# Gate projections of a hybrid diffusion layer moved in between the convolution tiles, and kept in DRAM until their merges

## The chip, the cores and the metric

The kernel is one program on one core of a Trainium2 chip. The metric is the device time of one execution in microseconds (us). Every time of an instruction below is from one profiled execution.

## The reference

Two token streams, 128 context tokens and 512 latent tokens, pass two layers with shared weights (D = 1024). Here both are one array of T = 640 columns. A layer is

```
h  = rmsnorm(x) * (1 + sc1) + sh1
proj = h @ w_in                       # q, k, v, z, b, a, the convolution's 3 x 512, Fourier's 512, 3 gates x 1024
y_a = delta_mixer(proj[q,k,v], z, b, a)         # gated DeltaNet, forward and backward, chunks of 64
y_b = hyena_mixer(proj[3 x 512])                # two long convolutions in the spectrum, gated
y_c = fourier_mixer(proj[512])                  # real part of a 2-D Fourier transform per group
g   = sigmoid(proj[gates])                      # three gates per channel
x  += g1 * ((g[0] * (y_a @ w_pa) + g[1] * (y_b @ w_pb) + g[2] * (y_c @ w_pc)) @ w_o)
x  += g2 * swiglu(rmsnorm(x) * (1 + sc2) + sh2)
```

and one last rmsnorm ends it. The outputs are both streams and the context's DeltaNet states.

## The kernel before

Activations lie transposed, 128 channels on the partitions and 640 tokens in the columns. A projection tile is 128 output channels: `gemm` makes it in two halves of 320 columns, each of 8 k-steps of three matmuls (the fp32 operands are split into a high and a low part, `mm3`), so 48 matmuls, into a PSUM tile named `pg`. Its weights come by one 512 KB load `wr` and are split into `wh` by ACT and `wl` by POOL (`wsplit`). A merge takes weights for two output tiles; a branch has four merges, 192 matmuls.

The source writes the foreground (projections, merges) as a plain sequence and everything else as coroutines (`bg`). After each quarter of a tile `pump` lets those coroutines issue a step whose inputs are ready by a cost model's clock; `finish` runs coroutines until they are done, with nothing of the foreground between. Each engine then executes its own list in that fixed order. SP issues nearly all transfers, in its own fixed order too.

In a layer's mixer (`mixer`) the order before is, after q, k and v: the delta block (`delta`: three batches of a triangular inverse on DVE, then the scan) starts in the background. The foreground is 4 Fourier tiles, stored to `fnS`; 4 z tiles, stored to `zS`; 12 convolution tiles (`proj_conv`: besides the matmuls four ACT copies and two DVE operations of 641 columns, stored to `hyS`); 8 gate tiles of branch a. I call this stretch the mix. Then `delta_out` (norm of the delta block's output, product with z) runs in the background of two gate tiles of branch c. Then the a merges with `fnet` (Fourier) in the background; the c merges with the other 6 c gates between them and `hyena` in the background; the 8 b gates, still with `hyena`; the b merges. I call the stretch from `delta_out` to the first b merge the tail. `hyena` is four passes (two halves of the channels, two orders): transposes, then five spectral stages, each with its own table load from `hT` and filter load from `kSp`, PE forward, DVE products, PE inverse; then two gated products.

The large SBUF tiles `A` come from a pool of 14, `T` (656 columns) from 6, `U` from 8.

Of the kernel before, what the change touches and what calls it, by code (L numbers as in the profile page):

```python
# [18 lines left out]
P = 128  # L19
D = 1024  # L20
# [4 lines left out]
T = TP + TS  # L25
NC = T // 2
# [14 lines left out]
OFF_HY = 2080  # L41
OFF_FN = 3616
OFF_G = 4128
QKV_ORDER = (4, 5, 6, 7, 0, 1, 2, 3, 8, 9, 10, 11)
BR = {"a": 0, "b": 1, "c": 2}
C_BMOD, C_G1, C_G2, C_CQ, C_CH, C_NA, C_FQ, C_B1, C_B2, C_NF = 0, 48, 56, 64, 100, 136, 137, 138, 139, 140
NPAR = 148


def _stream():  # L50
    s = [("ba", 0)] + [("in", m * P) for m in QKV_ORDER]
    s += [("in", OFF_FN + m * P) for m in range(4)]
    s += [("in", 1536 + m * P) for m in range(4)]
    s += [("in", OFF_HY + m * P) for m in range(12)]
    gate = lambda br, m: ("in", OFF_G + BR[br] * D + m * P)
    s += [gate("a", m) for m in range(8)]
    s += [gate("c", 0), gate("c", 1)]
    s += [("pa", m) for m in range(0, 8, 2)]
    s.append(("pc", 0))
    for m in range(2, 8, 2):  # L60
        s += [gate("c", m), gate("c", m + 1), ("pc", m)]
    s += [gate("b", m) for m in range(8)]
    s += [("pb", m) for m in range(0, 8, 2)]
# [235 lines left out]
class _Net:  # L299
# [138 lines left out]
                self.room -= c["pe"] - p  # L438
        self.last_pe = c["pe"]

    def finish(self, *cos):
        while True:
            cos = [co for co in cos if not co.done]
            if not cos:
                return
            self.finish_one(cos)

    def finish_one(self, cos):

# [193 lines left out]
    def setup(self):  # L643
        nc, I = self.nc, self.I
        sm = self.kp.tile([P, 1024], F32, name="small")
        nc.sync.dma_start(sm, I["small"])
        self.ident = sm[:, 0:128]
        self.ones = sm[:, 128:256]
        self.mask = sm[:, 256:384].rearrange("p (s i) -> p s i", s=2)
        self.inc = sm[:, 384:640].rearrange("p (s i) -> p s i", s=2)  # L650
        self.stc = sm[:, 640:896].rearrange("p (s i) -> p s i", s=2)
        self.parity = sm[:, 896:1024].rearrange("p (s i) -> p s i", s=2)
        sr = self.kp.tile([P, 256], F32R, name="stcr")
        nc.vector.tensor_copy(sr, sm[:, 640:896])
# [8 lines left out]
        self.hT = self.dr.tile([5, P, 2048], F32, name="hT")  # L663

    def load_par(self, l):
        nc = self.nc
# [387 lines left out]
    def proj_conv(self, key, wcol, l):  # L1054

        W = self.wget(key)
        cv = self.conv_tile(wcol, l)
        for c in range(2):
            self.proj(W, cv, c)
        return self.conv(cv)  # L1060

    def permute(self, dst, src, fn, goff=1):

# [668 lines left out]
            yield  # L1732


    def gates(self, l, br, dst):

        for m in range(8):
            self.gate(l, br, m, dst[m // 4][:, m % 4])

    def gate(self, l, br, m, dst):  # L1740
        W = self.wget(("in", OFF_G + BR[br] * D + m * P))
        for c in range(2):
            self.evict(dst, self.gemm(W, self.h, c, free=2), c, AF.Tanh, 0.5)
            self.pump()

    def merge(self, br, m, th, first, last):

        nc = self.nc
        W = self.wget(("p" + br, m))
        for i in range(2):  # L1750
            mt = self.mg[(m + i) // 4][:, (m + i) % 4]
# [21 lines left out]
    def mixer(self, l, co):  # L1773
        nc = self.nc
        v4 = lambda a: a.rearrange("p (m t) -> p m t", m=4)
# [11 lines left out]
        W = {}  # L1787
        for c in range(2):
# [3 lines left out]
            ps = self.gemm(W[-1], self.h, c, M=32, free=((1, 0), (0, 1))[c])  # L1792
# [29 lines left out]
        for m in range(4):  # L1822
            W = self.wget(("in", OFF_FN + m * P))
            t = self.Tt()
            for c in range(2):
                self.evict(t, self.gemm(W, self.h, c, free=2), c)
                self.pump()
            nc.sync.dma_start(self.fnS[m], t[:, :T])
        par = self.par[l][0]
        na = self.p2.tile([P, 1], F32, tag="na2", name=self.nm("na2"))  # L1830
        nc.vector.tensor_scalar(out=na, in0=par[:, C_NA:C_NA + 1], scalar1=0.5, scalar2=None, op0=ALU.mult)
        for m in range(4):
            W = self.wget(("in", 1536 + m * P))
            t, zm = self.Tt(), self.Tt()
            for c in range(2):
                ps = self.gemm(W, self.h, c, free=2)
                self.evict(t, ps, c, AF.Tanh, 0.5)
                sl = slice(c * NC, (c + 1) * NC)
                nc.vector.scalar_tensor_tensor(out=zm[:, sl], in0=t[:, sl], scalar=1.0, in1=ps[:, :NC],
                                               op0=ALU.add, op1=ALU.mult)  # L1840
                self.pump()
            nc.gpsimd.tensor_scalar(out=zm[:, :T], in0=zm[:, :T], scalar1=na, scalar2=1.0, op0=ALU.mult, op1=ALU.mult)
            nc.sync.dma_start(self.zS[m], zm[:, :T])
        self.mark(f'hy{l}')
        for m in range(12):
            o = self.proj_conv(("in", OFF_HY + m * P), C_CH + 3 * m, l)
            nc.sync.dma_start(self.hyS[m][:, 0:641], o)
        self.mark(f'ga{l}')
        while self.dst() is None:
            self.finish_one(gd)  # L1850
        self.mg = [v4(self.A()) for _ in range(2)]
# [12 lines left out]
        gh = self.bg(self.after(gf, self.hyena(l)))  # L1864
        mgv = [self.mg[m // 4][:, m % 4] for m in range(8)]
        for m in range(0, 8, 2):
            self.merge("a", m, mgv[m:m + 2], True, False)
        self.y["a"] = None
        self.mark(f'c{l}')
# [12 lines left out]
        self.h = None  # L1882
        self.mark(f'hfin{l}')
        self.finish(gh)
        self.mark(f'pb{l}')
        self.mgs = [[v4(self.A(F32R)) for _ in range(2)] for _ in range(2)]
        self.gm = self.bg(self.mods(l, (38, 40)[l], 48))
        for m in range(0, 8, 2):
            self.merge("b", m, [tb[(m + i) // 4][:, (m + i) % 4] for i in range(2)], False, True)
# [312 lines left out]
```

## Time and profile before

| | |
|---|---|
| median of 3 runs (lowest, highest) | 2847.31 us (2843.88, 2851.53) |
| profiled execution | 2847.94 us, of it 2846.2 us from the first to the last instruction |
| busy share | PE 91%, PEld 86%, DVE 66%, POOL 47%, ACT 36% |
| DMA | 324.24 MB, mean 114 GB/s |
| mean granted TensorE clock | 0.955 |

A line of the page or of an answer names tiles without their numbers: `pg` is a projection's or a merge's sum, `ps` any other PSUM tile, `hT`, `kSp`, `hyS`, `zS`, `fnS` are DRAM tensors. PE is the matmul itself, PEld its weight load. A granted clock of 1.00 is 2.4 GHz, and 0.5 is 1.2 GHz.

### The profile page before, as it was taken

The page shows a single profiled execution, that of the slowest core. Times are in us where ns is not written, and L with a number is a line of the kernel's source. Part 1 is how long each engine was busy: PE and PEld are TensorE (multiplying, and loading weights), DVE is VectorE, ACT ScalarE, POOL GpSimd, SP SyncE. Part 2 cuts the span into 40 slices and gives each one's busy share as a digit, 9 for nine tenths or more (in the row PEclk, how much of TensorE's full clock was granted, in tenths as well). Part 3 has the DMA queues.
Part 4 walks back from the last instruction along what each step waited for, and adds up shares of the span by engine and source line. Part 5 has one row for each costly group of instructions (what it writes and reads, how often), then busy time and mean ns, then how long its engine had stood idle before and what let it go on. Part 6 is the DMA issues. An engine that isn't in the chain of part 4 may idle for free. (4 is left out here: it accounts for less than half of the span.)

```text
span 2846.2 us, 56258 instructions
## 1 busy us (share of the span) xinstructions
PE 2595.5 (91%) x22664; PEld 2455.5 (86%) x22664; DVE 1870.7 (66%) x3504; ACT 1030.8 (36%) x2235; POOL 1331.2 (47%) x1228
## 2 busy tenths in 40 slices
PE   5798879898999999999988988799899999999998
PEld 3677778898999989999987777688889989999997
DVE  4466897844654585667765779876556457877765
ACT  2445223332233243344425542333323323444432
POOL 1242535333334465566633444354423345767662
PEclk9899989999999999999999999899999999999999
DMA  7432122243564336422222322213336442222222
GB/s 277 165 99 93 61 85 66 78 139 120 186 241 135 112 98 202 139 83 82 82 99 80 108 85 72 78 57 97 109 140 232 157 163 62 73 82 82 82 75 82
DMA packets 99957, 324.24 MB, mean 114 GB/s; under 512 B 10842, under 2 KB 25178, under 8 KB 93216
## 3 DMA queue, kind: packets, MB, share of 16 engines
q1 hardware_dynamic: 98256, 312.76, 33.2%
q0 software_dynamic: 1440, 7.87, 0.8%
q8 instruction: 179, 2.93, 0.4%
q14 instruction: 82, 0.67, 0.1%
HBM read 288.60 MB, written 37.24 MB: 114 GB/s over the span
## 5 line engine op out<-in xcount | busy, mean ns | idle before, releaser
L2151 PE MATMUL pg<-A,wh 128*128 128x320 f32 (+1 forms) x6304 | 1477.1, 321 | 53.7 <-DVE T L2151 14.8
L2151 PEld LDWEIGHTS pg<-A,wh 128*128 128x128 f32 (+1 forms) x6304 | 1081.6, 194 | 107.5 <-issue 22.3
L2151 POOL TENSOR_TENSOR wl<-wr,wh 128x512 fp32r<-128x512 f32 (+2 forms) x486 | 677.5, 1407 | 777.5 <-ACT wh L2151 745.4
L2151 PE MATMUL pg<-A,wl 128*128 128x320 f32 (+1 forms) x3152 | 997.9, 317 | 0.5 <-POOL wl L2151 0.4
L2151 PEld LDWEIGHTS pg<-A,wl 128*128 128x128 f32 (+1 forms) x3152 | 610.7, 194 | 3.6 <-POOL wl L2151 2.6
L2151 ACT CAST wh<-wr 128x512 fp32r<-128x512 f32 (+2 forms) x486 | 286.7, 612 | 416.1 <-PE pg L2151 306.7
L2151 PE MATMUL ps<-A,wh 128*128 128x320 f32 x1696 | 379.6, 310 | 0.0
L2151 PEld LDWEIGHTS ps<-A,wh 128*128 128x128 f32 x1696 | 283.4, 188 | 3.4 <-issue 2.4
L2151 PE MATMUL ps<-A,wl 128*128 128x320 f32 x848 | 263.6, 311 | 4.6 <-POOL wl L2151 4.3
L2151 PE MATMUL ps<-A,A 32*32 32x32 f32 (+5 forms) x2984 | 214.0, 249 | 51.7 <-DVE A L2151 50.0
L2151 POOL TENSOR_TENSOR wl<-U,wh 128x512 fp32r<-128x512 f32 x160 | 225.9, 1425 | 52.9 <-ACT wh L2151 52.9
L2151 PEld LDWEIGHTS ps<-A,A 32*32 32x32 f32 (+2 forms) x2984 | 185.4, 152 | 63.8 <-DVE A L2151 51.2
L2151 DVE TENSOR_TENSOR A<-A 128x120 f32<-128x120 f32 (+22 forms) x690 | 215.6, 376 | 10.5 <-DMA A<-hyS 7.6
L2151 DVE TENSOR_TENSOR T<-T,T 128x320 f32<-128x320 f32 (+1 forms) x139 | 133.4, 960 | 100.6 <-ACT T L2151 96.4
L2151 POOL TENSOR_TENSOR A<-A,A 128x640 fp32r<-128x640 f32 (+5 forms) x84 | 121.4, 1457 | 113.3 <-ACT A L2151 110.0
L2151 PE MATMUL pg<-A,A 128*128 128x320 f32 x1056 | 164.6, 313 | 6.2 <-ACT A L2151 5.7
L2151 PEld LDWEIGHTS ps<-A,wl 128*128 128x128 f32 x848 | 159.6, 188 | 7.2 <-POOL wl L2151 7.2
L2151 PEld LDWEIGHTS pg<-A,A 128*128 128x128 f32 x1056 | 158.0, 190 | 8.5 <-ACT A L2151 6.0
L2151 ACT CAST wh<-U 128x512 fp32r<-128x512 f32 x160 | 99.1, 621 | 153.8 <-PE pg L2151 59.9
L2151 DVE STREAM_TRANSPOSE A<-A 32x1024 f32<-32x1024 f32 x72 | 149.0, 2093 | 1.3
L2151 DVE TENSOR_TENSOR U<-ps,U 128x512 f32<-128x512 f32 x144 | 78.1, 543 | 102.9 <-PE ps L2151 64.7
L2151 POOL TENSOR_TENSOR A<-U,A 128x320 fp32r<-128x320 f32 (+1 forms) x48 | 53.8, 1127 | 165.1 <-ACT A L2151 165.1
(166 smaller groups left out, 3120.1 us busy)
## 6 DMA issues: line engine op xcount, KB each, us to landing
wr<-in_wbig_dram SPq DMA_DIRECT2D x272, 512.0 KB, 3.7
A<-in_wmod_dram SPq DMA_DIRECT2D x96, 512.0 KB, 4.4
A<-hT SPq DMA_DIRECT2D x32, 1024.0 KB, 8.7
kSp<-U SPq DMA_DIRECT2D x40, 256.0 KB, 2.1
U<-kSp SPq DMA_DIRECT2D x40, 256.0 KB, 9.1
hyS<-T SPq DMA_DIRECT2D x24, 320.5 KB, 3.1
wr<-in_wbig_dram SPq DMA_DIRECT2D x16, 384.0 KB, 3.1
T<-hyS SPq DMA_DIRECT2D x16, 320.5 KB, 5.7
```

Of the source, the lines that this page charges most:

```text
L2151: return f(*a, **k)
```

## The change

All 24 gate tiles of a layer are projected in the mix. A list `MIX` sets the order of its 44 tiles: 16 heavy ones (convolution and z) and, after each of them, one or two of 28 light ones (Fourier, then the gates of a, c and b). A gate goes to a `T` tile and is stored to a DRAM tensor `gS`; before its merges a branch's gates come back as two loads of 1280 KB into `A` tiles (`gated`). `fnet` and `hyena` are made coroutines after the last tile of `MIX`. `finish` may step further coroutines meanwhile (`also`).

```diff
+def _mix():
+    light = [("fn", m) for m in range(4)] + [(br, m) for br in "acb" for m in range(8)]
+    heavy = [("hy", m) for m in range(12)]
+    for i in range(4):
+        heavy.insert(4 * i + 2, ("z", i))
+    o = []
+    for i, k in enumerate(heavy):
+        o.append(k)
+        o += light[i * 28 // 16:(i + 1) * 28 // 16]
+    return o
...
-    def gate(self, l, br, m, dst):
-        W = self.wget(("in", OFF_G + BR[br] * D + m * P))
+    def gate(self, br, m):
+        t = self.Tt()
+        W = self.wget(("in", MIX_COL[br] + m * P))
         for c in range(2):
-            self.evict(dst, self.gemm(W, self.h, c, free=2), c, AF.Tanh, 0.5)
+            self.evict(t, self.gemm(W, self.h, c, free=2), c, AF.Tanh, 0.5)
             self.pump()
+        self.nc.sync.dma_start(self.gS[BR[br], m // 4, :, m % 4], t[:, :T])
+
+    def gated(self, br):
+        th = [self.A() for _ in range(2)]
+        for i in range(2):
+            self.nc.sync.dma_start(th[i], self.gS[BR[br], i].rearrange("p m t -> p (m t)"))
+        return [th[m // 4][:, (m % 4) * T:(m % 4 + 1) * T] for m in range(8)]
...
-        self.gates(l, "a", self.mg)
+        for n, (kind, m) in enumerate(MIX):
...
+            else:
+                self.gate(kind, m)
+        self.h = None
         self.mark(f'dfin{l}')
-        self.finish(*gd, *gm)
-        go = self.bg(self.delta_out(l))
-        th = []
-        for m in range(2):
-            th.append(self.Tt())
-            self.gate(l, "c", m, th[m])
-        self.finish(go)
-        self.mark(f'a{l}')
         gf = self.bg(self.fnet(l))
         gh = self.bg(self.after(gf, self.hyena(l)))
+        self.finish(*gd, *gm, also=[gf])
+        self.mg = self.gated("a")
+        go = self.bg(self.delta_out(l))
+        self.finish(go, also=[gf, gh])
+        self.mark(f'a{l}')
         for m in range(0, 8, 2):
-            self.merge("a", m, mgv[m:m + 2], True, False)
+            self.merge("a", m, self.mg[m:m + 2], True, False)
         self.y["a"] = None
+        th = self.gated("c")
+        self.finish(gf, also=[gh])
         for m in range(0, 8, 2):
-            if m:
-                th = [self.Tt() for _ in range(2)]
-                for i in range(2):
-                    self.gate(l, "c", m + i, th[i])
-            else:
-                self.finish(gf)
-            self.merge("c", m, th, False, False)
+            self.merge("c", m, th[m:m + 2], False, False)
         self.y["c"] = None
-        tb = [v4(self.A()) for _ in range(2)]
-        self.gates(l, "b", tb)
-        self.h = None
+        th = self.gated("b")
         self.finish(gh)
```

Three places in layer 0 show how the lists move. The first is PE in `hyena`'s third pass (before) and its third pass (after): `ps` with 256 columns are the spectral stages (`A_8571` and `A_9222` the transformed input, the `A` beside them a table, `U` a stage's products), `pg` are projections. Before:

```order
L2151 MATMUL ps_8810<-A_8608,U_8729 128x256
L2151 MATMUL ps_8811<-A_8608,U_8728 128x256 x2
L2151 MATMUL ps_8811<-A_8608,U_8729 128x256
L2151 MATMUL pg_8772<-A_464,wh_8632 128x320
L2151 MATMUL pg_8772<-A_466,wh_8632 128x320
L2151 MATMUL pg_8772<-A_464,wl_8633 128x320
L2151 MATMUL pg_8772<-A_464,wh_8632 128x320
L2151 MATMUL pg_8772<-A_466,wh_8632 128x320
L2151 MATMUL pg_8772<-A_464,wl_8633 128x320
L2151 MATMUL ps_8836<-A_8571,A_8766 128x256 x12
L2151 MATMUL pg_8772<-A_464,wh_8632 128x320
```

After:

```order
L2159 MATMUL ps_9298<-A_9242,U_9262 128x128 x2
L2159 MATMUL ps_9298<-A_9242,U_9263 128x128
L2159 MATMUL ps_9317<-A_9222,A_9250 128x256 x12
L2159 MATMUL ps_9342<-A_9246,U_9287 128x256 x2
L2159 MATMUL ps_9342<-A_9246,U_9288 128x256
L2159 MATMUL ps_9343<-A_9246,U_9287 128x256 x2
L2159 MATMUL ps_9343<-A_9246,U_9288 128x256
L2159 MATMUL ps_9342<-A_9246,U_9287 128x256 x2
L2159 MATMUL ps_9342<-A_9246,U_9288 128x256
L2159 MATMUL ps_9343<-A_9246,U_9287 128x256 x2
L2159 MATMUL ps_9343<-A_9246,U_9288 128x256
```

Before, half a gate's k-steps stand between two stages; after, the stages follow each other, and so it is for 372 matmuls in a row, the passes two to four, up to the first b merge.

The second is PE at the end of the mix: the five groups of `ps<-small,U` are the transposes of `delta_out`, `pg_6861` and `pg_6904` are halves of the gates c0 and c1, `pg_7799` is the second half of the last b gate, `pg_7952` the first a merge. Before:

```order
L2151 MATMUL pg_6861<-A_464,wh_6728 128x320
L2151 MATMUL pg_6861<-A_466,wh_6728 128x320
L2151 MATMUL pg_6861<-A_464,wl_6729 128x320
L2151 MATMUL ps_6895<-small,U_6855 128x128 x4
L2151 MATMUL pg_6904<-A_463,wh_6786 128x320
L2151 MATMUL pg_6904<-A_465,wh_6786 128x320
L2151 MATMUL pg_6904<-A_463,wl_6787 128x320
L2151 MATMUL pg_6904<-A_463,wh_6786 128x320
L2151 MATMUL pg_6904<-A_465,wh_6786 128x320
L2151 MATMUL pg_6904<-A_463,wl_6787 128x320
L2151 MATMUL ps_6913<-small,U_6857 128x128 x4
L2151 MATMUL ps_6919<-small,U_6859 128x128 x4
```

After:

```order
L2159 MATMUL pg_7799<-A_465,wh_7697 128x320
L2159 MATMUL pg_7799<-A_467,wh_7697 128x320
L2159 MATMUL pg_7799<-A_465,wl_7698 128x320
L2159 MATMUL ps_7879<-small,U_7873 128x128 x4
L2159 MATMUL ps_7887<-small,U_7875 128x128 x4
L2159 MATMUL ps_7895<-small,U_7877 128x128 x4
L2159 MATMUL ps_7901<-small,U_7885 128x128 x4
L2159 MATMUL ps_7907<-small,U_7893 128x128 x4
L2159 MATMUL pg_7952<-A_7913,wh_7760 128x320
L2159 MATMUL pg_7952<-A_7914,wh_7760 128x320
```

Before, the transposes stand inside two gate tiles; after, they stand alone between the last gate and the first merge.

The third is SP at the same place: `wr` are weights, `zS` is what `delta_out` multiplies by, `fnS` the input of `fnet`. Before:

```order
L2151 DMA wr_6740<-in_wbig_dram 128x1024
L2151 DMA wr_6803<-in_wbig_dram 128x1024
L2151 DMA A_6805<-zS 128x4x640
L2151 DMA wr_6911<-in_wbig_dram 128x1024
L2151 DMA A_7009<-fnS 128x4x640
L2151 DMA wr_7033<-in_wbig_dram 128x1024
```

After:

```order
L2159 DMA gS<-T_7770 128x640
L2159 DMA A_7834<-gS 128x2560
L2159 DMA A_7835<-gS 128x2560
L2159 DMA A_7838<-zS 128x4x640
L2159 DMA A_7857<-fnS 128x4x640
L2159 DMA U_7950<-in_nmid_dram 128x386
```

After, two gate loads of 1280 KB stand ahead of the load from `zS`, and the store of the last gate ahead of both.

Counted in PE's order, the last small matmul that runs beside the mix (of the delta block or of the modulation vectors) stands in layer 0 before the last 918 matmuls of the mix, in layer 1 before the last 756, all of them projections. The three triangular inverses' first matmuls stand after 12.5, 14.8 and 23.7 tiles of the mix before and after 12.4, 14.2 and 22.3 in layer 0; after 14.0, 16.2 and 24.4 before and 15.2, 17.0 and 25.7 in layer 1.

## Rows read from the trace of the kernel before

**Rows 1.** The page's first line.
```profile
span 2846.2 us, 56258 instructions
```

**Rows 2.** Windows: mix of layer 0, its tail, part of that, layer 1's, one waiting stretch.
```profile
core 0: us, PE busy (x) PEld busy (x) DVE busy (x) ACT busy (x) POOL busy (x), PEclk, DMA share, GB/s
278.00:619.00 341.00, 296.86 (x4372) 279.79 (x4371) 255.00 (x529) 109.14 (x261) 159.50 (x187) 0.91 0.26 80
619.00:892.00 273.00, 258.73 (x1830) 253.08 (x1829) 143.93 (x271) 85.88 (x192) 99.11 (x82) 0.97 0.48 166
639.00:697.00 58.00, 52.00 (x358) 48.54 (x356) 24.88 (x40) 17.83 (x41) 23.01 (x20) 0.97 0.31 97
1648.00:2006.00 358.00, 305.17 (x4378) 287.09 (x4377) 281.24 (x603) 120.93 (x284) 164.05 (x187) 0.90 0.23 73
2006.00:2282.00 276.00, 261.50 (x1830) 255.61 (x1829) 144.78 (x271) 85.97 (x191) 98.81 (x83) 0.96 0.47 164
400.00:425.00 25.00, 11.71 (x161) 11.14 (x161) 20.26 (x55) 7.89 (x20) 6.21 (x9) 0.59 0.23 74
```

**Rows 3.** Timeline, PE, 413 to 427: start, length, what; then idle before.
```profile
413.49 1.73 PE L2151 MATMUL ps<-A,A 32*32 32x32 f32 x62 [13.29 <-DVE A L2151]
...
419.68 0.73 PE L2151 MATMUL pg<-A,wh 128*128 128x320 f32 x2
...
421.28 0.73 PE L2151 MATMUL pg<-A,wh 128*128 128x320 f32 x2
...
425.24 0.45 PE L2151 MATMUL pg<-A,wh 128*128 128x320 f32 x2
...
426.12 0.45 PE L2151 MATMUL pg<-A,wh 128*128 128x320 f32 x2
```

**Rows 4.** Timeline, ACT and DVE, 619 to 642: output of the delta block.
```profile
619.26 2.70 ACT L2151 ACTIVATE U<-A 128x512 f32<-128x512 f32 x5
...
627.80 1.90 DVE L2151 TENSOR_TENSOR U<-A,osr 128x512 f32<-128x512 f32 x3
...
641.80 0.49 DVE L2151 SCALAR_TENSOR_TENSOR A<-A,pg 128x320 f32<-128x320 f32 x1 [0.66 <-PE pg L2151]
```

**Rows 5.** Timeline, DVE and PE, 647 to 697: Fourier block to the c merges.
```profile
647.49 3.45 DVE L2151 TENSOR_TENSOR A<-A 128x1020 f32<-128x1020 f32 x2
...
696.07 0.41 PE L2151 MATMUL pg<-A,wh 128*128 128x320 f32 x1 [1.14 <-ACT A L2151]
```

**Rows 6.** Timeline, SP, 690 to 830: where a convolution pass begins to load.
```profile
690.88 0.90 SPq L2151 DMA_DIRECT2D A<-hyS  x2
...
747.37 0.38 SPq L2151 DMA_DIRECT2D A<-hT  x1
...
794.08 0.38 SPq L2151 DMA_DIRECT2D A<-hT  x1
...
828.05 0.38 SPq L2151 DMA_DIRECT2D A<-hT  x1
```

**Rows 7.** Timeline, DVE and POOL, 839 to 872: the last pass.
```profile
839.25 0.69 DVE L2151 TENSOR_TENSOR U<-ps,U 128x512 f32<-128x512 f32 x1 [5.34 <-PE ps L2151]
...
841.24 0.75 DVE L2151 TENSOR_TENSOR U<-U,U 128x256 fp32r<-128x256 f32 x2
...
857.94 0.69 DVE L2151 TENSOR_TENSOR U<-ps,U 128x512 f32<-128x512 f32 x1 [1.93 <-POOL U L2151]
...
865.81 0.88 DVE L2151 TENSOR_TENSOR A<-A,T 128x128 f32<-128x128 f32 x2
...
868.55 2.94 POOL L2151 TENSOR_TENSOR A<-A,A 128x1280 fp32r<-128x1280 f32 x1 [4.08 <-ACT A L2151]
```

**Rows 8.** DMA issues: out<-in, engine, count, KB each, median us to landing.
```profile
A<-hT SPq DMA_DIRECT2D x32, 1024.0 KB, 8.7
...
A<-zS SPq DMA_DIRECT2D x2, 1280.0 KB, 6.6
```

More of the change, by code (lines that the diff above doesn't have):

```diff
@@ L44 @@
 QKV_ORDER = (4, 5, 6, 7, 0, 1, 2, 3, 8, 9, 10, 11)
-BR = {"a": 0, "b": 1, "c": 2}
+MIX_COL = {"fn": OFF_FN, "z": 1536, "hy": OFF_HY, "a": OFF_G, "b": OFF_G + D, "c": OFF_G + 2 * D}
+def _mix():
[8 more added lines that the diff above has]
+    return o
+MIX = _mix()
+BR = {"a": 0, "c": 1, "b": 2}
 C_BMOD, C_G1, C_G2, C_CQ, C_CH, C_NA, C_FQ, C_B1, C_B2, C_NF = 0, 48, 56, 64, 100, 136, 137, 138, 139, 140
@@ L51, in _stream @@
     s = [("ba", 0)] + [("in", m * P) for m in QKV_ORDER]
[L52 to L63, printed above, removed]
+    s += [("in", MIX_COL[k] + m * P) for k, m in MIX]
+    s += [("p" + br, m) for br in "acb" for m in range(0, 8, 2)]
     s += [("o", m) for m in range(8)]
@@ L439, in pump, with finish @@
         self.last_pe = c["pe"]
[L441 to L446, printed above, removed]
+    def finish(self, *cos, also=()):
+        while any(not co.done for co in cos):
+            self.finish_one([co for co in (*cos, *also) if not co.done])
     def finish_one(self, cos):
@@ L663, in setup @@
         self.hT = self.dr.tile([5, P, 2048], F32, name="hT")
+        self.gS = self.dr.tile([3, 2, P, 4, T], F32, name="gS")
     def load_par(self, l):
@@ L1060, in proj_conv, with to_fnet, to_gate @@
         return self.conv(cv)
+    def to_fnet(self, m):
+        W = self.wget(("in", OFF_FN + m * P))
+        t = self.Tt()
+        for c in range(2):
+            self.evict(t, self.gemm(W, self.h, c, free=2), c)
+            self.pump()
+        self.nc.sync.dma_start(self.fnS[m], t[:, :T])
+    def to_gate(self, m, na):
+        nc = self.nc
+        W = self.wget(("in", 1536 + m * P))
+        t, zm = self.Tt(), self.Tt()
+        for c in range(2):
+            ps = self.gemm(W, self.h, c, free=2)
+            self.evict(t, ps, c, AF.Tanh, 0.5)
+            sl = slice(c * NC, (c + 1) * NC)
+            nc.vector.scalar_tensor_tensor(out=zm[:, sl], in0=t[:, sl], scalar=1.0, in1=ps[:, :NC],
+                                           op0=ALU.add, op1=ALU.mult)
+            self.pump()
+        nc.gpsimd.tensor_scalar(out=zm[:, :T], in0=zm[:, :T], scalar1=na, scalar2=1.0, op0=ALU.mult, op1=ALU.mult)
+        nc.sync.dma_start(self.zS[m], zm[:, :T])
     def permute(self, dst, src, fn, goff=1):
@@ L1732, in hyena @@
             yield
-    def gates(self, l, br, dst):
-        for m in range(8):
-            self.gate(l, br, m, dst[m // 4][:, m % 4])
-    def gate(self, l, br, m, dst):
-        W = self.wget(("in", OFF_G + BR[br] * D + m * P))
+    def gate(self, br, m):
+        t = self.Tt()
+        W = self.wget(("in", MIX_COL[br] + m * P))
         for c in range(2):
-            self.evict(dst, self.gemm(W, self.h, c, free=2), c, AF.Tanh, 0.5)
+            self.evict(t, self.gemm(W, self.h, c, free=2), c, AF.Tanh, 0.5)
             self.pump()
+        self.nc.sync.dma_start(self.gS[BR[br], m // 4, :, m % 4], t[:, :T])
[4 more added lines that the diff above has]
+        return [th[m // 4][:, (m % 4) * T:(m % 4 + 1) * T] for m in range(8)]
     def merge(self, br, m, th, first, last):
@@ L1750, in merge @@
         for i in range(2):
-            mt = self.mg[(m + i) // 4][:, (m + i) % 4]
+            mt = self.mg[m + i]
             for c in range(2):
@@ L1821, in mixer @@
         self.mark(f'fn{l}')
[L1822 to L1829, printed above, removed]
-        na = self.p2.tile([P, 1], F32, tag="na2", name=self.nm("na2"))
-        nc.vector.tensor_scalar(out=na, in0=par[:, C_NA:C_NA + 1], scalar1=0.5, scalar2=None, op0=ALU.mult)
@@ L1832, in mixer @@
[L1832 to L1851, printed above, removed]
-        gm = [self.bg(self.when_met(self.dpr, self.mods(l, (MODS1, 34)[l], (38, 40)[l])))]
-        self.gates(l, "a", self.mg)
-        self.mark(f'dfin{l}')
-        self.finish(*gd, *gm)
@@ L1856, in mixer @@
-        go = self.bg(self.delta_out(l))
-        th = []
-        for m in range(2):
-            th.append(self.Tt())
-            self.gate(l, "c", m, th[m])
-        self.finish(go)
-        self.mark(f'a{l}')
+        na = self.p2.tile([P, 1], F32, tag="na2", name=self.nm("na2"))
+        nc.vector.tensor_scalar(out=na, in0=self.par[l][0][:, C_NA:C_NA + 1], scalar1=0.5, scalar2=None, op0=ALU.mult)
+        gm = [self.bg(self.when_met(self.dpr, self.mods(l, (MODS1, 34)[l], (38, 40)[l])))]
+        for n, (kind, m) in enumerate(MIX):
+            if n in (11, 22, 33):
+                self.mark(f'mix{n}_{l}')
+            if kind == "fn":
+                self.to_fnet(m)
+            elif kind == "z":
+                self.to_gate(m, na)
+            elif kind == "hy":
+                o = self.proj_conv(("in", OFF_HY + m * P), C_CH + 3 * m, l)
+                nc.sync.dma_start(self.hyS[m][:, 0:641], o)
+            else:
+                self.gate(kind, m)
@@ L1888, in mixer @@
         for m in range(0, 8, 2):
-            self.merge("b", m, [tb[(m + i) // 4][:, (m + i) % 4] for i in range(2)], False, True)
+            self.merge("b", m, th[m:m + 2], False, True)
         self.y["b"] = None
```

3 lines of the change are left out of this document (1 added, 2 removed).

## The prediction

> **What bounds the kernel now.** I read the page first for the span [rows 1], then windows cut where the work changes, because the share of PE over the whole span hides two different stages. In the mix of layer 0 PE is busy 296.86 of 341 us, so it stands idle for 44.1 us, and DVE is busy 255; in layer 1 it is 305.17 of 358, idle 52.8 [rows 2]. In the tail PE is busy 258.73 of 273 and 261.50 of 276, idle 14.3 and 14.5 [rows 2]. So the tail is bound by PE, and the mix nearly so. Then the timeline of PE for the mix's idle time: the largest piece is 13.29 us before the first inverse's matmuls, released by DVE [rows 3]. That is a chain on DVE, not a want of matmuls ahead: PE works its list in order, and the small matmul stands at its head. After that gap six projection matmuls take 1.60 us (419.68 to 421.28), later 0.88 (425.24 to 426.12): 0.267 and 0.147 us each, the lower and the full clock [rows 3].
>
> **The change part by part.**
>
> *Gate tiles leave the tail.* 16 tiles a layer (8 of c, 8 of b) of 48 matmuls are 768 matmuls; at 0.147 us [rows 3] that is 112.7 us of PE, beside which the tail's other work ran. The work itself is not removed, only moved.
>
> *They enter the mix.* The mix grows by 112.7 us, less the idle time that they fill. They could fill at most 44.1 and 52.8 us. But the order of PE shows that the inverses stand behind nearly as many tiles as before (12.5, 14.8, 23.7 against 12.4, 14.2, 22.3 in layer 0): what changed is which tiles these are, and the extra 16 come after the delta block, where nothing is left that waits. What the change does give the delta block is a freer DVE, since fewer convolution tiles, with two DVE operations each, stand before the third inverse (about 6 instead of 12). I take 8 us off in layer 0; in layer 1, where the inverses stand one tile (7 us) later than before, 10. The mix grows by 104.7 and 102.7. Bounds: 112.7 less all idle time, 68.6 and 59.9, and 117 if stores add waits of their own.
>
> *Stores and reloads.* 24 stores of 320 KB and 6 loads of 1280 KB a layer. The stores lie beside matmuls, with the 16 DMA engines busy for 0.26 of the mix [rows 2]; each waits on ACT's eviction of the same tile, and SP's next weight load stands behind it. The Fourier, z and convolution tiles of before store in the same way, and a weight load goes two tiles ahead, so I take nothing; without this cover a tile would lose a few us, which the bound of 117 holds only in part and the range must. The loads count where they stand ahead of others, in the next two items.
>
> *delta_out loses its cover.* Before, from the first square at 619.26 to the first a merge's product at 641.80, less the 12 matmuls of that product (1.8 us), is 20.7 us, in which two c gates ran [rows 4]. Now PE has 20 transposes there. The load from `zS` also stands behind two gate loads of its own size: one alone lands in 6.6 us [rows 8], three in 6.6 to 19.8; I take 16. The first product with z could start some 10.4 us after the first square (the normed tiles start at 627.80 and come 0.6 us apart, and a transpose is between [rows 4]), so the chain waits up to 9 us. I take 4 and get 24.5 us; 20 to 30 are the ends.
>
> *a merges with Fourier.* Before from 640.0 to 696.07, 56 us, in which `fnet` starts 7.5 us late, at 647.49 [rows 5]; PE is busy for 52 of 58 [rows 2]. No gate was between, so only the start moves: its first DVE operations now stand right behind delta_out's. 51 us; 46 to 58.
>
> *First convolution pass with the c merges.* Before, its first load is at 690.88 and the next pass begins to load at 747.37 [rows 6]: 51 us after the c merges' start at 696.07 [rows 5], with c gates between. Without these it is shorter, but the loads of c's gates stand ahead of its first load on SP. I take 42; 35 to 51.
>
> *Passes two to four alone.* In the order these are 372 matmuls in a row with no projection between. Before, the passes begin to load at 747.37, 794.08 and 828.05 [rows 6], and the last split for the b merges ends at 871.49 [rows 7]: 124.1 us. The parts of the last pass: 11.2 us from its first table load to its first product, four steps of 4.67 (839.25 to 857.94), 8.75 from the last product to the end of the gated ones, 4.8 for the split [rows 7]. A pass has its own chain: a table lands in 8.7 us [rows 8], DVE needs 2.74 of each step (839.25 to 841.99 [rows 7]), and ACT, POOL and PE stand between. Matmuls of gates no longer delay it, so steps fall to about 4, and the load for the second half of the channels can be issued earlier than the 46.7 us of the second pass suggest. I take 36 a pass and 5 for the split: 113 us. Lower end: five steps of 2.74, 8.7 and 8.75 make 31 a pass, 95 in all; upper end: three passes of 46.7, 140.
>
> *The tail's sum* is 24.5 + 51 + 42 + 113 = 230.5 us against 273 and 276: 42.5 and 45.5 less, though 112.7 of PE's work is gone. PE's idle time in it rises from 14 to about 85 us. With the ends of all items it is 196 to 279.
>
> *Sum.* Layer 0: 104.7 - 42.5 = 62.2. Layer 1: 102.7 - 45.5 = 57.2. Together 119.4 on the profiled execution's own 2847.94 (span 2846.2 [rows 1]), which stands 0.6 above the median of the runs, 2847.31: 2967 us. All before the mix, after the b merges and in the FFN is the same list on every engine and costs nothing more.
>
> **Rivals.**
>
> *The chain alone is faster than I think.* With no gates on PE and more `A` tiles free, the tables of a pass may be loaded during the one before. Then a pass is near its lower end, 31, and the first hides wholly beside the c merges: tail 205, mix 98.7 and 96.7. That is 98.7 - 68 + 96.7 - 71 = 56: 2904 us. For it: DVE works only 2.74 of each 4.67 us, and waited for PE in between [rows 7]. Against it: a pass cannot transform before the pass ahead has made its input, and 8 `U` tiles hold its filters and products.
>
> *The clock falls in the tail.* After the gap of 13.29 us the granted clock of that stretch is 0.59, and matmuls cost 0.267 instead of 0.147 for about 8 us [rows 2, 3]. Alone, a pass lets PE wait for tables and for each step's products. At the lower clock its 114 transform matmuls of up to 256 columns cost 0.8 x 0.120 = 0.096 us more each, 11 a pass, 35 for 3.2 passes, of which I put 24.5 on the chain: tail 255. 104.7 - 18 + 102.7 - 21 = 168: 3016 us. Against it: gaps of one to five us in the mix leave a mean of 0.91 [rows 2]. The Trainium skill, "TensorE: Matmul & The Clock Gate", section "HAM oscillation — how this bites in real kernels", says that short runs of matmuls between waits for loads are throttled again at every wait. [rows 3] agree for one wait; by that rule the time is this rival's.
>
> *Faster: the gates fill the mix's waits.* If the moved tiles take in all of the idle 44.1 and 52.8 us, the mix grows by only 68.6 and 59.9. The tail must then be under 204 in layer 0 and 216 in layer 1 for a gain; at its lower end, 197, it is 68.6 - 76 + 59.9 - 79 = -26.5: 2821 us. For it: DVE holds PE up in the mix, and gates need no DVE. Against it: the extra tiles stand behind the waits in the order, not ahead of them.
>
> *No change*: growth and shrinkage cancel, at tails near 170 us with my mix. Nothing in the rows speaks for it.
>
> **How the numbers follow.** The forecast 0.58, the faster chain 0.19, the lower clock 0.15, filled waits 0.05, no change 0.03. Within 0.3% (8.5 us, about what a measurement of this kernel can tell from no change) is 0.03, faster 0.05, slower 0.92. The items' ends together (the mix by 59.9 to 117, the tail by 196 to 279) would give 2817 to 3090, but they don't fall together. The range 2890 to 3030 holds the forecast with about a third of its tail's spread, nearly all of the faster chain, and the middle of the lower clock.
>
> **What would show it.** Right, if in the changed kernel: the mix lasts some 445 us and ends with over 100 us in which PE is busy throughout while DVE does next to nothing; PE is idle for about 20 us around delta_out's transposes; and `hyena` runs some 110 us with PE busy under half, at a granted clock between 0.6 and 0.9. The step on the mix is wrong if the mix grows by under 90 us; the step on the passes is wrong if three of them take under 95 or over 130. The forecast fails as a whole if the tail falls below 170 us, or if weight loads begin to wait behind the gate stores, which would show as idle time of PE before projections, released by POOL or ACT, in the mix's last 100 us.

## The result, and the profile after

The changed kernel takes 2963.57 us (median of 4 runs, 2957.9 to 2967.33), against 2847.93 us in the runs beside them; the ratio is 1.0399, with a 95% interval of 1.038 to 1.0417. It is slower by 4%, and the time is 3.4 us under the forecast of 2967.

The page's first line, to be read beside [rows 1]:

```profile
span 2962.3 us, 56405 instructions
```

The program gained 116.1 us. The windows of the changed kernel, cut where the work changes as in [rows 2]: mix and tail of layer 0, then of layer 1, then three parts of layer 0 (the mix's last 120 us, delta_out, the passes two to four):

```profile
core 0: us, PE busy (x) PEld busy (x) DVE busy (x) ACT busy (x) POOL busy (x), PEclk, DMA share, GB/s
280.00:735.00 455.00, 408.03 (x5119) 389.66 (x5117) 251.91 (x528) 142.12 (x326) 209.40 (x214) 0.93 0.30 95
735.00:956.00 221.00, 173.87 (x1076) 157.06 (x1080) 135.94 (x271) 55.81 (x126) 58.09 (x51) 0.85 0.57 211
1712.00:2175.00 463.00, 419.23 (x5148) 401.99 (x5146) 269.14 (x604) 154.21 (x349) 206.04 (x215) 0.93 0.29 92
2175.00:2396.00 221.00, 174.53 (x1072) 158.54 (x1072) 136.07 (x271) 56.01 (x126) 57.98 (x51) 0.83 0.57 211
615.00:735.00 120.00, 118.79 (x810) 118.53 (x809) 10.29 (x12) 38.79 (x86) 46.19 (x53) 1.00 0.38 122
735.00:767.00 32.00, 13.59 (x56) 11.38 (x56) 21.90 (x36) 8.40 (x18) 10.09 (x11) 0.68 0.55 206
862.00:950.00 88.00, 67.22 (x378) 58.94 (x378) 62.25 (x137) 21.32 (x53) 14.18 (x17) 0.78 0.65 246
```

Three things are to be seen. The mix grew by over 100 us a layer and ends with 120 us in which PE is busy for 118.79 and DVE for 10.29: pure projections, beside which only their own evictions, products and weight splits run (ACT 38.79, POOL 46.19). The tail shrank by only 53 us (55 in layer 1), and PE is now idle in it for 47 us (221 less 173.87) where it was 14 [rows 2]. And the granted clock of the tail fell from 0.97 to 0.85.

For a sum without rounding, two instructions mark each layer: the first square of `delta_out` (ACT) and the product of the first b merge (DVE). In layer 0 of the changed kernel, timelines of ACT and then of DVE (start, length, what):

```profile
734.59 2.70 ACT L2159 ACTIVATE U<-A 128x512 f32<-128x512 f32 x5
```

```profile
766.90 0.47 DVE L2159 SCALAR_TENSOR_TENSOR A<-A,pg 128x320 f32<-128x320 f32 x1
...
956.04 0.49 DVE L2159 SCALAR_TENSOR_TENSOR A<-A,pg 128x320 f32<-128x320 f32 x1 [6.05 <-PE pg L2159]
```

The square stood at 619.26 [rows 4], the b product of the kernel before at 893.28:

```profile
893.28 0.49 DVE L2151 SCALAR_TENSOR_TENSOR A<-A,pg 128x320 f32<-128x320 f32 x1 [26.60 <-PE pg L2151]
```

Between the marks, in us:

| stretch | before | after | difference |
|---|---|---|---|
| start to first square, layer 0 | 619.3 | 734.6 | +115.3 |
| tail of layer 0 | 274.0 | 221.5 | -52.6 |
| b merges to first square, layer 1 | 1112.7 | 1218.6 | +105.9 |
| tail of layer 1 | 277.0 | 221.6 | -55.4 |
| to the end | 563.2 | 566.1 | +2.8 |

The sum is +116.1. All of the loss but 2.8 us lies in the stretches where the gates came from and where they went; the cause of the 2.8 stays open.

### The profile page after: what moved, and what is told of

Same layout as the page of the kernel before. It is cut to its first block, busy times and chain, and to the rows that moved or that the text cites. A ratio compares the mean times of both kernels' runs of the same rounds, so it can differ in the third digit from the quotient of the medians.

```text
span 2962.3 us, 56405 instructions
## 1 busy us (share of the span) xinstructions
PE 2647.5 (89%) x22664; PEld 2488.6 (84%) x22664; DVE 1839.6 (62%) x3504; ACT 1036.1 (35%) x2235; POOL 1340.7 (45%) x1228
## 5 line engine op out<-in xcount | busy, mean ns | idle before, releaser
L2159 POOL TENSOR_TENSOR wl<-wr,wh 128x512 fp32r<-128x512 f32 (+2 forms) x486 | 693.7, 1439 | 883.3 <-ACT wh L2159 868.8
L2159 PE MATMUL ps<-A,A 32*32 32x32 f32 (+5 forms) x2984 | 228.9, 254 | 39.3 <-DVE A L2159 31.6
L2159 PEld LDWEIGHTS ps<-A,A 32*32 32x32 f32 (+2 forms) x2984 | 196.8, 156 | 55.7 <-DVE A L2159 34.1
L2159 DVE SCALAR_TENSOR_TENSOR T<-T,par,T 128x641 f32<-128x641 f32 x84 | 102.0, 1214 | 192.3 <-ACT T L2159 142.4
L2159 DVE TENSOR_TENSOR A<-A 128x120 f32<-128x120 f32 (+20 forms) x690 | 204.1, 360 | 3.1
L2159 ACT COPY U<-ps 128x128 f32<-128x128 f32 (+2 forms) x176 | 67.4, 385 | 187.8 <-PE ps L2159 186.0
```

The lines of the kernel that those rows point to most:

```text
L2159: return f(*a, **k)
```

## The experiments

### Is it the cover or the round trip through DRAM? All three chains covered again, all gates still through DRAM

The mix is in the old order, then come the gates of c and b, stored to `gS` and reloaded as in the changed kernel; the three chains (`delta_out`, `fnet`, `hyena`) start as background of these gates.

```diff
-    light = [("fn", m) for m in range(4)] + [(br, m) for br in "acb" for m in range(8)]
...
+    return [(k, m) for k, n in (("fn", 4), ("z", 4), ("hy", 12), ("a", 8), ("c", 8), ("b", 8)) for m in range(n)]
...
+            if n == 20:
+                go = self.bg(self.after(gd[1], self.delta_out(l)))
+                gf = self.bg(self.after(go, self.fnet(l)))
+                gh = self.bg(self.after(gf, self.hyena(l)))
...
-        gf = self.bg(self.fnet(l))
-        gh = self.bg(self.after(gf, self.hyena(l)))
...
```

> All 24 gate tiles of a layer still go through DRAM, with the same stores and reloads, but the order of the mix is Fourier, z, convolution, then the gates of a, c and b, and delta_out, fnet and hyena are background of these gates instead of following them. Theory (the added time is the cover that the tail lost, not the round trip): PE has 768 matmuls a layer beside the chains again, so the time falls back to about 2850 us, between 2835 and 2870. Rival 1 (stores and reloads through DRAM cost the time): it stays above 2920. Rival 2 (gates take in waiting time of the mix that before could not): under 2835.

2847.8 us, ratio to before 0.9997 (0.9985 to 1.0009). The 48 stores of 320 KB and 12 loads of 1280 KB are all there, and the added time is gone. Its windows in layer 0, up to the first square, and from there on the stretch with all three chains, the gates of c and b and most of the merges:

```profile
281.00:605.00 324.00, 279.93 (x4275) 262.69 (x4274) 251.82 (x526) 104.00 (x250) 152.27 (x180) 0.92 0.28 90
605.00:894.00 289.00, 271.23 (x1910) 264.87 (x1909) 142.08 (x271) 88.54 (x197) 104.46 (x86) 0.98 0.55 200
```

PE is idle for 44.1 and 17.8 us; before it was 44.1 in the mix and 14.3 in the tail [rows 2]. So stores and reloads cost nothing that can be measured when the chains are covered: the interval leaves them at most some 3 us. The run also puts the mix back into its old order, but that order is not where the loss was: PE idles 47.0 and 43.8 us in the mixes of the changed kernel, 44.1 and 52.8 before [rows 2]. The loss was in the main the cover; 13.6 us of it come from where the reloads stand on SP, as the run on the load order below shows.

The other end: before's order and before's tail, with only the a gates through DRAM.

```diff
-    light = [("fn", m) for m in range(4)] + [(br, m) for br in "acb" for m in range(8)]
...
+    return [(k, m) for k, n in (("fn", 4), ("z", 4), ("hy", 12), ("a", 8)) for m in range(n)]
...
+        self.finish(*gd, *gm)
+        self.mg = self.gated("a")
+        go = self.bg(self.delta_out(l))
+        th = []
+        for m in range(2):
+            th.append(self.Tt())
+            self.gate_at("c", m, th[m])
+        self.finish(go)
...
```

> Gates of c and b are projected in the tail as in the kernel before, straight into SBUF; the mix is in the order of before; only the 8 gates of a go through DRAM (8 stores, 2 loads a layer). Theory: 2847 us, between 2838 and 2858, with PE idle for about 44 and 53 us in the two mixes and 14 in the tails. Rival (a store costs the weight load that stands behind it on SP a wait): 16 stores at 1 us or more, 2863 and above.

2853.58 us, ratio 1.0019 (1.001 to 1.0028): inside the range, though not equal. PE idles 44.9 and 50.8 us in the mixes, 16.0 and 16.5 in the tails. The trace has a likely reason: the first product of `delta_out` waits for the load from `zS`, which stands behind two gate loads on SP, although two c gates run beside it. From the first square to the first a product it is 28.5 us in layer 0 and 25.8 in layer 1, against 22.5 and 22.2 before.

```profile
632.73 0.69 DVE L2171 TENSOR_TENSOR A<-ps,A 128x512 f32<-128x512 f32 x1 [3.84 <-DMA A<-zS]
```

### Part of the cover back: the b gates beside the passes

`gate_at` is the `gate` of before: it projects a gate into an SBUF tile.

```diff
-    light = [("fn", m) for m in range(4)] + [(br, m) for br in "acb" for m in range(8)]
+    light = [("fn", m) for m in range(4)] + [(br, m) for br in "ac" for m in range(8)]
...
-        th = self.gated("b")
+        th = [self.A() for _ in range(2)]
+        th = [th[m // 4][:, (m % 4) * T:(m % 4 + 1) * T] for m in range(8)]
+        for m in range(8):
+            self.gate_at("b", m, th[m])
+        self.h = None
         self.finish(gh)
```

> The changed kernel with the 8 b gates of a layer projected after the c merges again, beside hyena, straight into SBUF; a and c as in the changed kernel. On PE the list now has the third pass and the one ahead of it between these gates, and 136 small matmuls, the last pass, alone behind them. Theory (what counts is PE's work beside the passes): the mix gets 56 us shorter a layer (384 matmuls at 0.147 us), the stretch from the c merges to the b merges grows from 94 to about 123 us, as eight gates of 7.05 us hold two passes and one pass stays alone: 27 us less a layer, 2909 us, between 2890 and 2925. Rival (the time is lost at delta_out and by the reloads, not in the passes): 2955 or more.

2899.15 us, ratio 1.0185 (1.0161 to 1.0208). The tails grew by 29.1 and 30.4 us against the changed kernel, as expected (29); the stretches ahead of them shrank by 70.0 and 56.1, where 56 was expected. In layer 0 PE also idles 9.6 us less in the mix (384.6 less 347.59 against 454.59 less 408.03), which the theory did not have. So with eight gates beside the passes the kernel gets back 64 of 116 us, where 54 were expected. The last pass, alone in PE's list, still shows its wait of 4.13 us:

```profile
881.68 0.44 PE L2170 MATMUL ps<-small,A 128*128 128x128 f32 x2 [4.13 <-DVE A L2170]
```

### Is the lower clock part of the price?

In the changed kernel each pass ends with a wait of PE for the gated products, and the granted clock behind it is 0.50. PE's timeline where the passes two, three and four begin, then windows at the start of the second (PE alone: us, busy, granted clock, DMA share, GB/s):

```profile
865.74 2.57 PE L2159 MATMUL ps<-small,A 128*128 128x128 f32 x10 [3.89 <-DVE A L2159]
...
892.68 2.57 PE L2159 MATMUL ps<-small,A 128*128 128x128 f32 x10 [3.77 <-DVE A L2159]
...
922.36 2.57 PE L2159 MATMUL ps<-small,A 128*128 128x128 f32 x10 [3.89 <-DVE A L2159]
```

```profile
866.00:870.00 4.00, 3.28 (x13) 0.50 1.01 401
870.00:874.00 4.00, 4.00 (x20) 0.50 0.32 132
874.00:878.00 4.00, 3.43 (x26) 0.93 0.33 100
```

Ten transposes take 2.57 us at 1.2 GHz (a granted clock of 0.50), and they take as long behind all three waits. Passes follow each other in 26.9 and 29.7 us. The first run fills the waits at the passes' ends:

```diff
+    def fill(self, n):
+        ps = self.gps()
...
+        for i in range(n):
+            self.nc.tensor.transpose(ps[:, 0:P], self.ident, self.ident)
...
                 yield from self.stagger([one(ft) for ft in (4, 0, 1, 2, 3)], 3)
...
+                self.fill(28)
...
```

> The changed kernel, with 28 transposes of a constant (0.129 us each at the full clock, 3.6 us) put on PE after the last inverse matmuls of each of hyena's four passes, where PE waited 3.9 us; their results are not used. No other instruction changes its place. Theory (of the added time about half is PE at the lower clock after these waits: matmuls of 128x256 take 0.24 instead of 0.13 us in the first 10 us of a pass): the granted clock between the passes stays at 1.00, each of the passes two to four gets about 4 us shorter, the b merges' start 3, so 15 us a layer: 2933 us, between 2925 and 2945. Rival (the passes are bound by the chain through DVE, ACT and POOL, and PE's clock is hidden under it): 2960 to 2968.

2959.76 us, ratio 1.0397 (1.0378 to 1.0416): no change against the changed kernel. My theory of half the loss in the clock fell with this run. The clock had risen only in part: from 874 to 878 it was 0.67 again, so a second run filled the inner waits too:

```diff
+                    if ft in (4, 0, 1):
+                        self.fill(6 if ft == 4 else 4)
                     px = self.ps()
...
+                    if ft in (4, 0):
+                        self.fill(5)
```

> As the run with 28 transposes at each pass's end, and further ones (6, 4 and 4 ahead of the first three forward products of a pass, 5 ahead of the first two inverse ones, 0.13 us each), so that PE does not wait inside the first two steps of a pass either, where in that run its clock still fell to 1.2 GHz some 8 us into the pass. Theory now (passes two to four are bound by the chain through DVE, ACT and POOL, the lower clock lies under it): the granted clock of the passes rises further and the time stays between 2952 and 2966. Rival (the lower clock after each wait is on the path, the first run only moved it): 2945 or less.

2959.0 us, ratio 1.039 (1.0368 to 1.0412). The same window of the three kernels, first with 28 transposes, then with all fillers; the changed kernel's is the last row of its windows above, at 0.78:

```profile
862.00:950.00 88.00, 72.20 (x479) 63.69 (x477) 60.94 (x134) 21.98 (x53) 15.04 (x17) 0.92 0.64 240
```

```profile
862.00:950.00 88.00, 75.62 (x573) 67.77 (x571) 63.11 (x139) 23.64 (x57) 17.47 (x19) 1.00 0.67 249
```

At a clock of 1.00 throughout, the passes follow each other in 26.5 and 26.7 us (transposes at 868.12, 894.66 and 921.37):

```profile
894.66 0.44 PE L2171 MATMUL ps<-small,A 128*128 128x128 f32 x2 [0.70 <-DVE A L2171]
...
902.22 0.44 PE L2171 MATMUL ps<-A,U 128*128 128x128 f32 x2 [0.45 <-ACT U L2171]
903.07 1.00 PE L2171 MATMUL ps<-A,U 128*128 128x128 f32 x7 [0.42 <-POOL U L2171]
```

With the full clock in the passes the tails are 3.3 and 4.7 us shorter; PE, twice as fast, then waits for ACT, DVE and POOL instead. The whole stays within 5 us of the changed kernel, and the intervals of the ratios overlap. Whether the fillers themselves cost something was not separated; that PE still waits 0.70 us for DVE right behind the 28 transposes speaks against it at that place.

### The load order at delta_out

```diff
+        go = self.bg(self.delta_out(l))
...
+        self.step(go)
...
         self.mg = self.gated("a")
-        go = self.bg(self.delta_out(l))
...
```

The step issues the load from `zS`. The cost model's landing times of these three loads were set to those of the changed kernel, so that nothing else moves.

> The changed kernel with the load from zS issued ahead of the two gate loads of branch a; no other instruction changes its place. In the changed kernel the third of these loads lands 13.7 us after its issue, and the first product with z stands 7.1 us (layer 0) and 5.6 us (layer 1) behind its transposes. Theory (the wait is the place in SP's order): it lands about 7 us after its issue, both waits go, delta_out takes 24 instead of 31 us: 2951 us, between 2948 and 2956. Rival (the three loads share the same DMA engines, so the order is nothing): 2961 to 2965.

2949.97 us, ratio to before 1.0354 (1.0335 to 1.0373); 13.6 us below the changed kernel. The median landing of `zS`, of the changed kernel and then of this one:

```profile
A<-zS SPq DMA_DIRECT2D x2, 1280.0 KB, 13.7
```

```profile
A<-zS SPq DMA_DIRECT2D x2, 1280.0 KB, 6.7
```

These loads, issued back to back by SP, land in the order of their issue: `zS` after 13.7 us as the third and after 6.7 as the first, `fnS`, the fourth in both kernels, after 15.8 and 15.7. The wait that went, in the changed kernel's timeline of DVE:

```profile
749.84 0.69 DVE L2159 TENSOR_TENSOR A<-ps,A 128x512 f32<-128x512 f32 x1 [7.08 <-DMA A<-zS]
```

### Can gates take in the waits of the mix?

The round trip allows the a gates before z and convolution, so that DVE is freer for the first inverse. Twice: with all gates through DRAM and the chains covered, and with before's tail (and the load from `zS` first). The list of the first, against that of the run with the chains covered (the chains start at its tile 28 instead of 20); the second has it without c and b:

```diff
-    return [(k, m) for k, n in (("fn", 4), ("z", 4), ("hy", 12), ("a", 8), ("c", 8), ("b", 8)) for m in range(n)]
+    return [(k, m) for k, n in (("fn", 4), ("a", 8), ("z", 4), ("hy", 12), ("c", 8), ("b", 8)) for m in range(n)]
```

> The run whose gates all go through DRAM and cover the chains again, with another order in the mix: Fourier, the 8 gates of a, z, convolution, then c and b. Only the round trip through DRAM allows the a gates this early, since SBUF has no place for them while the delta block runs. Theory (PE waits in the mix for DVE, and z and convolution tiles bring DVE about 1 and 2.4 us each): some 13 us of DVE's work leave the stretch ahead of the first inverse, where PE waits 12.9 us, and the products of z no longer stand behind the inverse's operations: 8 to 13 us a layer less, 2830 us, between 2820 and 2838. Rival (DVE has the same sum of work, so the wait comes back at the third inverse): 2843 to 2852.

> The same order of the mix (Fourier, a gates through DRAM, z, convolution), but the c and b gates in the tail as in the kernel before, straight into SBUF, and the load from zS ahead of the gate loads. Theory: the same gain in the mix, 2830 us, between 2820 and 2840. Rival: 2845 to 2853.

2845.3 us, ratio 0.9994 (0.9983 to 1.0005), and 2854.31 us, ratio 1.0027 (1.0017 to 1.0037). No gain came: the first time is the rival's, the second 1.3 us above the rival's range, though `delta_out` to the first a product is back at 23.2 us in layer 0 with the load from `zS` first. But the rival's reason, a wait that comes back at the third inverse, is not what the trace shows. PE at the first inverse, first in the kernel with all gates through DRAM in the old order, then with the a gates early:

```profile
411.81 1.73 PE L2149 MATMUL ps<-A,A 32*32 32x32 f32 x62 [12.92 <-DVE A L2149]
```

```profile
404.20 1.73 PE L2149 MATMUL ps<-A,A 32*32 32x32 f32 x62 [24.82 <-DVE A L2149]
```

DVE's chain did end 7.6 us sooner. But the matmul stands behind about as many tiles as before (23.5 against 24.6, counted from the program's start), these tiles ran without the short waits of z and convolution, and PE came to it 19.5 us sooner. So it would be the place of the waiting matmul in the list that sets the wait. The next runs move that place, and with it what follows in the delta block, by 14 us of the cost model, in three kernels: before, all gates through DRAM and covered, and the same with the a gates early.

```diff
+            if mixed and (p, a) == quads[-1]:
+                self.cur.t += 14.0
             yield 0 if (p, a) == quads[-1] else 1.5
```

> The kernel before, with the ready time of the first inverse's first matmuls put 14 us later in the cost model, so that they stand 2 tiles of projections (96 matmuls) later in PE's list. Theory (PE's wait of 13.3 and 14.4 us there comes from the place in the list; tiles that stand ahead of the waiting matmul fill it, tiles behind it can't, which is why the changed kernel's 16 tiles a layer did not shorten the mix's idle time): both waits go, less 2 to 4 us that come back further on: 2847 - 24 = 2823 us, between 2817 and 2833. Rival (the delta block ends later by as much, and the wait comes back at the second and third inverse or before delta_out): 2843 to 2853.

> The same edit in the kernel whose gates all go through DRAM and cover the chains. Theory: 2824 us, between 2817 and 2834; a delta block that ends later costs nothing here, since the 16 gates of c and b can stand beside it. Rival: 2843 to 2853.

> The same edit with the a gates ahead of z and convolution, where PE waited 24.8 and 22.2 us before the first inverse. Theory: 14 us of each wait go: 2845 - 26 = 2819 us, between 2812 and 2832. Rival: 2840 to 2850.

2841.33 us, ratio 0.9978 (0.9964 to 0.9992); 2837.26 us, 0.9958 (0.9942 to 0.9973); 2853.84 us, 1.0011 (0.9998 to 1.0024). PE at the first and the second inverse in the second of them, then at the second inverse in the same kernel without the edit:

```profile
420.05 1.11 PE L2151 MATMUL ps<-A,A 32*32 32x32 f32 x64
424.28 2.21 PE L2151 MATMUL ps<-A,A 32*32 32x32 f32 x64 [2.04 <-ACT A L2151]
...
443.09 3.62 PE L2151 MATMUL ps<-A,A 32*32 32x32 f32 x126 [7.84 <-DVE A L2151]
```

```profile
447.28 3.62 PE L2149 MATMUL ps<-A,A 32*32 32x32 f32 x126 [4.10 <-DVE A L2149]
```

The wait of 12.92 us at the first inverse is down to 2.04, but the one at the second grew from 4.10 to 7.84, and the mix's idle time fell only from 44.1 to 37.4 us (window of 281 to 620: 339 less 301.60). A gain of 24 us was expected of the first two, and 6 to 13 came, between theory and rival. With the a gates early nothing was gained, and the time is above the rival's range too: in layer 0 the wait at the first inverse fell from 24.82 to 14.29, but PE then waits 4.92 us for a product of z (21.08 in layer 1) and 7.54 at the second inverse (3.41 without the edit), and it idles 47.0 us in the mix with the edit and without. The second kernel is faster than both kernels of this case. It projects the gates in the mix and keeps them in DRAM as the change does, but with the chains beside them.

## Why the prediction held, term by term

The terms are those of the prediction. In layer 0 of the changed kernel they are divided by the first square (734.59), the first a product less 1.8 us (765.1), the start of the c merges (814.0), the second pass's first table load (848.9) and the first b product less 1.8 (954.2).

| term (layer 0, layer 1) | forecast | measured |
|---|---|---|
| mix grows | 104.7, 102.7 | 115.3, 105.9 |
| delta_out, to the first a product less 1.8 | 24.5 | 30.5, 29.3 |
| a merges with Fourier | 51 | 48.9, 48.7 |
| first pass with the c merges | 42 | 34.9, 36.6 |
| passes two to four and split | 113 | 105.3, 105.3 |
| tail | 230.5 | 219.6, 219.8 |

The mechanism was right: the gates' 112.7 us of PE moved and did not vanish, and what had run beside them stood alone. The run with all gates through DRAM and the chains covered shows it from the other side. But the total is closer than its terms, and that is luck: the forecast had the mix 13.8 us too small, the tails 21.6 too large, and these partly cancel; what is left of the 116.1 us are 2.8 at the end of the program, which I took as unchanged, and 1.7 from where the windows were cut.

**The mix.** "I take 8 us off in layer 0", and 10 in layer 1. In layer 0 PE's idle time did not fall at all, 44.1 to 47.0 (455 less 408.03), in layer 1 it fell by 9.1 (52.8 to 43.8). The wait at the first inverse stayed, 13.29 us before [rows 3]:

```profile
413.52 1.73 PE L2159 MATMUL ps<-A,A 32*32 32x32 f32 x62 [12.35 <-DVE A L2159]
```

The later gain that I forecast was there: before the third inverse PE waited 4.81 and 3.65 us, now 2.48. What ate it are three waits of over 1 us that PE did not have in the mix of before: 4.67 us for POOL, told below, 2.78 for a copy of ACT and 2.06 for a load of modulation weights. The products of z cost about what they cost before, in another place. They stand behind the inverse's operations on DVE while PE waits for them: once for 8.35 us in the changed kernel, before in four waits of 3.34, 1.45, 1.21 and 1.99. The changed kernel, then the kernel before:

```profile
351.29 0.90 PE L2159 MATMUL pg<-A,wh 128*128 128x320 f32 x2 [8.35 <-DVE T L2159]
```

```profile
339.90 0.90 PE L2151 MATMUL pg<-A,wh 128*128 128x320 f32 x2 [3.34 <-DVE T L2151]
```

That the gates could not take in the waits was forecast for the right reason: the extra tiles stand behind the waits. The last runs bear this out in part, since moving the waiting matmul back shortens its wait, and about half of what was expected, or nothing, is left of it in the time.

**delta_out.** I allowed 4 us for the load from `zS`, out of up to 9. It was 7.08 and 5.90. With the load first, delta_out takes 24.5 us in layer 0 (734.12 to 760.37, less 1.8). That is the forecast's figure, but without any wait for the load, of which the forecast held 4 us: so the term was 2 to 3 us short on the load and about 3 short on the rest of the chain. PE's idle time there, 18.4 us in the window of 735 to 767, is as forecast (about 20):

```profile
741.62 2.82 PE L2159 MATMUL ps<-small,U 128*128 128x128 f32 x12 [7.83 <-DVE U L2159]
751.19 2.31 PE L2159 MATMUL ps<-small,U 128*128 128x128 f32 x8 [6.75 <-DVE U L2159]
755.04 0.64 PE L2159 MATMUL pg<-A,wh 128*128 128x320 f32 x1 [1.54 <-ACT A L2159]
```

**The passes.** "I take 36 a pass and 5 for the split: 113 us", with a lower end of 31 a pass. It was 105.3: 16.8 us from the first table load to the second pass's transposes, then 26.9 and 29.7 from pass to pass, then 31.9 for the last with the split. From pass to pass this is below the lower end, because that end counted a table's landing, 8.7 us, into every pass. (Three times 31 with the split is 98; the prediction's 95 has most of the split left out.) In the changed kernel the tables of a pass are issued while the one before still runs: the third pass's first at 881.66, 11 us ahead of its transposes at 892.68.

```profile
881.66 0.41 SPq L2159 DMA_DIRECT2D A<-hT  x1
...
888.76 0.59 SPq L2159 DMA_DIRECT2D A<-hT  x1
```

That was the first rival's reason (2904 us), and in this it was right; the time was still nearer to the forecast, since the mix and delta_out cost more. The first pass, beside the c merges, was as much too large, 42 us where it was 34.9 and 36.6, about its lower end of 35; why is open.

**The lower clock.** The rival of 3016 us had its sign in the trace, a clock of 0.78 in the passes, and not its price: with the full clock in the passes a layer's tail is under 5 us shorter. The Trainium skill, "TensorE: Matmul & The Clock Gate", section "HAM oscillation — how this bites in real kernels", says that matmuls between waits for loads run throttled after each wait. The trace agrees about the clock, with ten transposes in 2.57 us after each of three waits of 3.77 to 3.89 us. It does not follow that the time grows by what the matmuls lose: here most of it lay under the chain through DVE, ACT and POOL.

Two of the prediction's signs did not come out for the same reason. PE was to be idle for about 85 us in the tail, and it was 47; in the passes it was to be busy under half, and it was busy for 67.22 of 88 us. PE's work in the tail of before, 258.73 us, less the gates' 112.7 is 146; in the changed kernel it is busy for 173.87, at a granted clock of 0.85. So some 28 us of what I took for idle time are matmuls that last longer: a busy share says little about what bounds a stretch as long as the clock is low.

**Filled waits** (2821 us) did not come about, and the stores show no wait of their own where nothing else runs: in the last 120 us of the mix, with a store for each tile, PE is busy for 118.79.

## What to carry to other kernels

Work that needs only the bottleneck engine is cover: its worth is what runs beside it, so before it is moved, look at which chain loses it and whether the new place has a wait ahead of which, not behind which, it will stand. In an in-order list, tiles behind a waiting matmul do not fill its wait; tiles ahead of it do, but here about half of what that gains, or all of it, came back at later waits. A round trip through DRAM is free only where its loads do not stand ahead of one that a chain waits for. A low clock in a stretch is a price only if PE is what the stretch waits for; fill the gaps once and see.

## What the runs showed of the hardware

A POOL instruction can be held up for many DVE instructions in a row. In the mix of the changed kernel one weight split on POOL, mean 1.44 us on the page, took 13.07 us while DVE ran a dense row of small operations with two SBUF inputs; PE then waited 4.67 us for it. Timelines of POOL, DVE (up to 516) and PE:

```profile
505.45 13.07 POOL L2159 TENSOR_TENSOR wl<-wr,wh 128x512 fp32r<-128x512 f32 x1 [6.46 <-ACT wh L2159]
```

```profile
504.75 11.45 DVE L2159 TENSOR_TENSOR A<-A 128x96 f32<-128x96 f32 x59
```

```profile
518.57 0.64 PE L2159 MATMUL pg<-A,wl 128*128 128x320 f32 x1 [4.67 <-POOL wl L2159]
```

Spans on POOL are rough, but PE's wait confirms this one. The Trainium skill, "SBUF — State Buffer", section "SBUF: two separate sides", says that such a DVE operation and a POOL operation that reads SBUF exclude each other: whichever starts first has the port pair that both share for its whole instruction. Here POOL did not get its turn at the end of one DVE instruction; it waited over dozens of them. From 517.3 on the two take turns, as by that section: within the same row of DVE the next splits last 1.3 us each, and each DVE operation beside them 1.3 us where it took 0.25 until then. POOL, then DVE, from 518.5 to 521:

```profile
518.48 2.53 POOL L2159 TENSOR_TENSOR wl<-wr,wh 128x512 fp32r<-128x512 f32 x2
```

```profile
518.55 2.56 DVE L2159 TENSOR_TENSOR A<-A 128x84 f32<-128x84 f32 x2
```

It is no product of the change alone: the longest split of the kernel before takes 7.90 us. Only argued, not tested: that DVE's next instruction takes the port again before POOL can; what let POOL in at 517.3 is open.
